# Every second pair of expert units loaded through POOL's queue instead of SyncE's

## The chip, the cores and the metric

The kernel runs on one core of a Trainium2 chip. The metric is the device time of one execution in microseconds; before the change it was 1349.06 us, the median of three runs (1348.57 to 1350.34). All data are fp32.

## The reference

One decoder layer on 256 tokens of width 1024: a mixer of three branches with an output projection, cross-attention to 256 memory tokens, and a mixture of experts, each followed by a residual sum and a LayerNorm. The change touches the mixture of experts alone:

```python
logits = hf @ router_w + router_b                # 32 experts, the top 4 of each token
act = clamped_swiglu(xb @ w_gu[e] + b_gu[e])     # w_gu[e]: 1024 x 2048
yb = act @ w_down[e] + b_down[e]                 # w_down[e]: 1024 x 1024
acc = acc.at[tok].add(yb * gate)
```

The weights of the 32 experts are 403 MB, and every expert is used, so all of them have to come from HBM once.

## The kernel before

The layer's dense part comes first (its weights are called raw when they are loaded, and whl when they are split into two parts). Then the experts run one after the other, each for up to 64 tokens. An expert's weights are cut into 12 **units** of 128 x 2048 numbers, 1.05 MB: units 12e to 12e+7 are for the up projection (two halves of four units, psum hp), 12e+8 to 12e+11 for the down projection (psum yp). PE reads the units strictly in their order, 0 to 383. Two neighbouring units that begin with an even number stand together in HBM as one block, a **pair**, and are loaded by one DMA of 128 rows of 16 KB, 2 MB (line 829).

A loaded unit stands in a **home**, a buffer in SBUF. The first 22 units (NF = 22) are placed by FIRST (line 87), partly during the dense part. From unit 22 on, later_chunks() (line 95) walks round the list WRAP (line 89): the homes ra0, ra1, re0, re1, rab, C, P, A and Q hold a pair each, the four of ONES (raw, two whl and rb) a single unit, and these four are left out from unit 120 on. So a round has 22 units at first and 18, nine pairs, later.

What sets the order of the loads: behind each unit's matmuls the program calls used(n) (line 1104). It takes the next loads off the list `waiting` as long as the home of the first one held no unit later than n, and hands each to chunk_load (line 817). The load is a DMA instruction in the order of the engine that issues it. There it waits until PE has really read the old units of the home, and, since there are eight semaphores for the landings of an engine's loads, until the load eight places before it on that engine has landed. All this stands on SyncE (SP): single units at line 827, the halves of units for the home raw and for the last four units at line 815, pairs at line 829.

POOL has little to do from the experts' beginning on: at expert 12 it loads the bias rows bd (lines 1431 and 1432), which the sums acc need at expert 14 (acc_bias, line 1263); at expert 16 stands overflow() (line 1275), a branch that is taken only when an expert has more than 64 tokens, with loads on POOL's queue inside (when it isn't taken, POOL brings the semaphores of its loads to where the branch would have left them, INC_SWDGE_SEM at line 1280); and in the last LayerNorm it does two instructions on the tile o. Every engine goes through the test of the branch.

Of the kernel before, what the change touches and what calls it, by code (L numbers as in the profile page):

```python
# [90 lines left out]
NF = 22  # L91
# [73 lines left out]
def trunk(ctx, tc, xT, xn, mem, wd, wm, bdn, par, rows, out, upto=None):  # L165
    nc = tc.nc
    clock = {"pe": 6.0, "dve": 4.0, "act": 4.0, "step": 0, "hold": 0}
    POOL, SP = nc.gpsimd, nc.sync
# [31 lines left out]
    wpair = wm.rearrange("(n j) p c -> n (j p c)", j=2).rearrange("n (p x) -> n p x", p=128)  # L200
# [587 lines left out]
    def src(n, a, b):  # L788

        o = (n % 2) * UW  # L790
        return wpair[n // 2, :, o + a:o + b]
# [9 lines left out]
    homes = {"rab": rab}  # L801

    def place(h, n, i):

        if h not in homes:
            homes[h] = new_home(h)
        t = homes[h]
        if h == "raw":
            ring[n] = t
        else:  # L810
            v = t if h in ONES else t[:, i]
            ring[n] = [v[:, k * D:(k + 1) * D] for k in range(2)]

    def half_load(n, k):
        SP.dma_start(out=ring[n][k], in_=src(n, k * D, (k + 1) * D))

    def chunk_load(h, units, fresh=True):
        if fresh:
            homes.pop(h, None)
        for i, n in enumerate(units):  # L820
            place(h, n, i)
        if h == "raw" or units[-1] >= NW - 4:
            for n in units:
                for k in range(2):
                    half_load(n, k)
        elif len(units) == 1:
            SP.dma_start(out=homes[h], in_=src(units[0], 0, UW))
        else:
            SP.dma_start(out=homes[h].rearrange("p j c -> p (j c)"), in_=wpair[units[0] // 2])

    def sigm(p, arg, o):
        ACT.activation(o, p, AF.Sigmoid, bias=pc("b_in", arg))
# [185 lines left out]
    for u in range(NU):  # L1018
        kind, arg = ORDER[u]
        if u in EARLY:  # L1020
            n, k = divmod(EARLY[u], 2)
            if k == 0:
                h, us = next((h, us) for h, us in FIRST if n in us)
# [73 lines left out]
    for h in ("raw", f"whl{S3}", f"whl{S2}", "rb", "A"):  # L1097
        chunk_load(*waiting.popleft())
# [5 lines left out]
    def used(n):  # L1104

        while waiting and holds[waiting[0][0]] <= n:
            h, us = waiting.popleft()
            chunk_load(h, us)
            holds[h] = us[-1]
# [65 lines left out]
    def ypt():  # L1175
        return mq.tile([128, 512], FP, name="yp", tag="yp")
# [165 lines left out]
    for e in range(NE):  # L1342
# [24 lines left out]
        if e == 0:  # L1367
            keep_warm(hp0, WARM[3])
            banks = [ypt(), misc("xgp"), hp1]

            def first(k):
                gather(xg, G, banks[k % 3], k, 1, (0, 1))

            first(0)
            first(1)
            chunk_load(*last_chunk)
            residual_rows(0)
            residual_rows(1)
            for k in range(8):
                up_part(hp0, xs, [ring[k // 2][k % 2]], [k])  # L1380
                if k < 6:
                    first(k + 2)
                if k % 2:
                    used(k // 2)
        else:
            for q in range(4):
                up(hp0, 0, q)
                if e == ROWS3_AT:
                    a, h = divmod(q, 2)
                    p = ypt()  # L1390
                    PE.matmul(p, ones, diag[:, 4 * q:4 * q + 4, :].rearrange("p n c -> p (n c)"), start=True, stop=True)
                    ACT.activation(r3[:, a, h * 512:(h + 1) * 512], p, AF.Copy)
# [3 lines left out]
        for q in range(4):  # L1396
# [5 lines left out]
            if e == NE - 1:  # L1402
                c, h = divmod(q, 2)
# [175 lines left out]
```

## Time and profile before

| | |
|---|---|
| median of three runs | 1349.06 us |
| the profiled execution | 1349.69 us |
| its span, first to last instruction | 1348.0 us |
| PE, DVE, ACT busy | 1274.3, 539.2, 427.4 us |
| POOL busy | 7.6 us |
| moved by DMA | 478.87 MB, 355 GB/s over the span |
| of it SP's queue (q1) | 474.41 MB in 54416 packets |
| of it POOL's queue (q0) | 2.76 MB in 784 packets |

One execution was profiled. Its span lies inside its own time; what remains is before the first and after the last instruction. A busy PE is not a PE at its peak, since matmuls overlap. The page also cuts the span into 40 slices and gives, for each, the busy share of the engines and what the DMA moved; a window query gives the same for any stretch. The chain is followed back from the last instruction: at each step to what released it. A DMA in the chain lasts from its issue to its landing. "DMA share" is the mean busy share of the core's 16 DMA engines.

### The profile page before, as it was taken

How to read it: one execution, taken by the hardware profiler on the slowest of the kernel's cores; microseconds unless marked ns; L12 is line 12 of the kernel's file. 1: busy time of each engine (PE TensorE's matmuls, PEld its weight loads, DVE VectorE, ACT ScalarE, POOL GpSimd, SP SyncE). 2: the span in 40 equal slices, each digit the busy share in tenths (PEclk: the TensorE clock that was granted, in tenths of full speed). 3: DMA queues.
4: the chain of work that ended last, by engine and by line, in shares of the span. 5: the costliest groups of instructions: out<-in, count | busy, mean ns of one | idle time of the engine just before them, and what ended most of it. 6: DMA issues, size and time to landing. Idle time of an engine off the chain costs nothing. (4 is left out here: it accounts for less than half of the span.)

```text
span 1348.0 us, 17416 instructions
## 1 busy us (share of the span) xinstructions
PE 1274.3 (95%) x7063; PEld 718.0 (53%) x7064; DVE 539.2 (40%) x1022; ACT 427.4 (32%) x841; POOL 7.6 (1%) x30
## 2 busy tenths in 40 slices
PE   9999999999999999999999989899999998889896
PEld 8999799988896343343333333343343333333332
DVE  6898889868754322222122121212222122222213
ACT  6878798764654111111111111112111011111101
POOL 0000000000000000000000000000000000000000
PEclk9999999999999999999999998999999999999998
DMA  6766576467679999999999999999999999999994
GB/s 213 238 205 231 188 236 201 144 197 242 235 257 378 409 428 426 427 425 423 419 428 428 426 429 427 426 426 428 427 428 428 428 426 428 428 428 427 427 427 169
DMA packets 55574, 478.87 MB, mean 355 GB/s; under 512 B 6560, under 2 KB 6816, under 8 KB 31424
## 3 DMA queue, kind: packets, MB, share of 16 engines
q1 hardware_dynamic: 54416, 474.41, 87.7%
q0 software_dynamic: 784, 2.76, 0.6%
q8 instruction: 58, 0.95, 0.3%
q10 hardware_dynamic: 288, 0.52, 0.1%
q14 instruction: 28, 0.23, 0.0%
HBM read 476.61 MB, written 1.05 MB: 354 GB/s over the span
## 5 line engine op out<-in xcount | busy, mean ns | idle before, releaser
L160 PE MATMUL hp<-ring,xg 128*64 128x512 f32 x2040 | 458.6, 597 | 20.3 <-DMA ring<-in_wm 16.6
L160 PEld LDWEIGHTS hp<-ring,xg 128*64 128x64 f32 x2040 | 143.7, 137 | 302.6 <-issue 267.1
L160 PE MATMUL yp<-ring,act 128*64 128x512 f32 x1016 | 239.6, 603 | 19.1 <-DMA ring<-in_wm 18.6
L160 PE MATMUL pd<-x_hl,whl 128*128 128x256 f32 x1896 | 232.0, 284 | 1.3 <-ACT whl L160 1.3
L160 DVE TENSOR_TENSOR hb<-hT,par 128x512 f32<-128x512 f32 x64 | 44.3, 692 | 471.1 <-PE hT L160 459.1
L160 PEld LDWEIGHTS pd<-x_hl,whl 128*128 128x128 f32 x1896 | 229.1, 192 | 2.2 <-ACT whl L160 1.9
L160 DVE TENSOR_TENSOR whl<-raw,whl 128x1024 fp32r<-128x1024 f32 x117 | 142.9, 1222 | 41.6 <-ACT whl L160 40.7
L160 PEld LDWEIGHTS yp<-ring,act 128*64 128x64 f32 x1016 | 67.6, 137 | 143.8 <-issue 140.4
L160 ACT ACTIVATE whl<-raw 128x1024 fp32r<-128x1024 f32 x117 | 123.5, 1056 | 48.4 <-DMA raw<-in_wd 21.3
L160 ACT ACTIVATE hs<-hp 128x256 f32<-128x256 f32 x128 | 42.1, 381 | 274.0 <-PE hp L160 274.0
L160 ACT ACTIVATE sg<-hb 128x256 f32<-128x256 f32 x64 | 26.7, 417 | 259.9 <-DVE hb L160 259.9
L160 ACT ACTIVATE cprod<-u,par 128x256 f32<-128x256 f32 x198 | 85.0, 498 | 0.0
L160 DVE COPY ys<-yp 64x512 f32<-64x512 f32 x31 | 21.5, 693 | 155.1 <-ACT ys L160 155.1
L160 PE MATMUL hp<-G,yn 128*128 128x128 f32 x488 | 59.0, 279 | 12.8 <-DVE G L160 12.8
L160 PEld LDWEIGHTS hp<-G,yn 128*128 128x128 f32 x488 | 55.8, 192 | 27.6 <-DVE G L160 26.0
L160 DVE TENSOR_TENSOR q_t<-q_t,cprod 128x512 f32<-128x512 f32 x99 | 65.5, 686 | 1.0
L160 PE MATMUL acc<-ys,GT 128*128 128x512 f32 (+1 forms) x128 | 60.0, 607 | 0.0
L160 PEld LDWEIGHTS hT<-ident,hs 128*128 128x128 f32 x256 | 26.8, 140 | 51.9 <-issue 50.3
L160 ACT ACTIVATE xg<-hp,lnp 128x128 f32<-128x128 f32 x62 | 28.4, 458 | 71.3 <-PE hp L160 56.9
L160 DVE TENSOR_SCALAR xg<-hp,lnp 128x128 f32<-128x128 f32 x60 | 24.6, 410 | 62.0 <-ACT xg L160 62.0
L160 ACT ACTIVATE ys<-yp 64x512 f32<-64x512 f32 x31 | 18.3, 590 | 91.1 <-PE yp L160 91.1
L160 PEld LDWEIGHTS acc<-ys,GT 128*128 128x128 f32 (+1 forms) x128 | 22.7, 189 | 36.3 <-issue 36.3
(221 smaller groups left out, 836.5 us busy)
## 6 DMA issues: line engine op xcount, KB each, us to landing
ring<-in_wm SPq DMA_DIRECT2D x173, 2048.0 KB, 36.2
raw<-in_wd SPq DMA_DIRECT2D x130, 512.0 KB, 4.2
ring<-in_wm SPq DMA_DIRECT2D x42, 512.0 KB, 8.1
ring<-in_wm SPq DMA_DIRECT2D x15, 1024.0 KB, 21.3
rab<-in_wm SPq DMA_DIRECT2D x4, 512.0 KB, 5.6
memn<-in_mem SPq DMA_DIRECT2D x1, 1024.0 KB, 7.2
q_t<-in_xn POOLq DMA_DIRECT2D x1, 1024.0 KB, 6.1
rab<-in_rows POOLq DMA_DIRECT2D x2, 512.0 KB, 7.8
```

Source lines behind the costliest of these rows:

```text
L160: return f(*args, **kw)
```

## The change

In chunk_load, a pair from unit 22 on whose first number doesn't divide by 4 is issued by POOL; the pairs with 24, 28, 32 and so on stay on SP, and so do single units, half units and the first 22 units.

```diff
         elif len(units) == 1:
             SP.dma_start(out=homes[h], in_=src(units[0], 0, UW))
         else:
-            SP.dma_start(out=homes[h].rearrange("p j c -> p (j c)"), in_=wpair[units[0] // 2])
+            queue = POOL if units[0] >= NF and units[0] % 4 else SP
+            queue.dma_start(out=homes[h].rearrange("p j c -> p (j c)"), in_=wpair[units[0] // 2])
```

## Rows read from the trace of the kernel before

**Rows 1.** The page: busy time of the engines, share of the span, instructions.

```profile
PE 1274.3 (95%) x7063; PEld 718.0 (53%) x7064; DVE 539.2 (40%) x1022; ACT 427.4 (32%) x841; POOL 7.6 (1%) x30
```

**Rows 2.** Stretches: length, engines' busy time, PE clock, DMA share, GB/s.

```profile
455.00:640.00 185.00, 180.26 (x878) 71.18 (x876) 43.01 (x101) 28.07 (x69) 0.00 (x0) 1.00 1.01 424
...
670.00:860.00 190.00, 178.56 (x824) 67.12 (x820) 39.41 (x94) 25.49 (x64) 0.00 (x0) 0.98 1.01 427
860.00:1020.00 160.00, 152.77 (x709) 60.42 (x708) 35.72 (x92) 24.00 (x58) 0.00 (x0) 0.99 1.01 427
1020.00:1314.00 294.00, 264.44 (x1246) 100.23 (x1244) 59.69 (x140) 37.83 (x93) 0.00 (x0) 1.00 1.01 427
```

**Rows 3.** DMA from 1020 to 1300 us: queues; issues, us to landing.

```profile
DMA packets 8219, 119.71 MB, mean 428 GB/s; under 512 B 911, under 2 KB 911, under 8 KB 911
...
q1 hardware_dynamic: 8207, 119.54, 100.4%
q8 instruction: 9, 0.15, 0.2%
...
ring<-in_wm SPq DMA_DIRECT2D x53, 2048.0 KB, 39.1
```

**Rows 4.** SP's waits, 455 to 1286 us: total us, times, longest.

```profile
SPq L829 <- DMA ring<-in_wm: 381.7, 113, 5.0
SPq L829 <- PE hp L160: 173.9, 65, 7.6
```

**Rows 5.** The chain that ended last: start, us, what.

```profile
1278.43 36.99 DMA ring<-in_wm
...
1328.39 7.04 PE yp L160 x32
```

**Rows 6.** SP's issues of ring loads: ns (minimum, median, maximum).

```profile
L829 SPq DMA_DIRECT2D ring<-in_wm x173: 327/328/424, 417.3 to 1281.9; - x173
```

**Rows 7.** The timeline of POOL: start, us, instruction.

```profile
407.96 0.53 POOL L1061 DMA_DIRECT2D gain<-in_rows  x1 [73.59 <-DMA ring<-in_wm]
```

**Rows 8.** The timeline of SP from 428 to 431 us.

```profile
429.15 0.33 SPq L829 DMA_DIRECT2D ring<-in_wm  x1
```

**Rows 9.** DMA from 430.5 to 433.5 us: packets, MB, share.

```profile
q1 hardware_dynamic: 71, 0.90, 76.2%
```

**Rows 10.** DMA issues over the whole span: KB, us to landing.

```profile
raw<-in_wd SPq DMA_DIRECT2D x130, 512.0 KB, 4.2
...
q_t<-in_xn POOLq DMA_DIRECT2D x1, 1024.0 KB, 6.1
...
gain<-in_rows POOLq DMA_DIRECT2D x1, 512.0 KB, 8.2
```

**Rows 11.** DMA from 411.7 to 415.8 us, both queues at work.

```profile
DMA packets 311, 1.75 MB, mean 428 GB/s; under 512 B 33, under 2 KB 33, under 8 KB 161
...
q1 hardware_dynamic: 167, 1.23, 71.0%
q0 software_dynamic: 144, 0.52, 31.3%
```

**Rows 12.** The tile bd: who reads it, and its loads.

```profile
L160 PE MATMUL acc<-bd,gT x8: 589/688/1057, 832.9 to 836.9; 33*128 33x512 f32 x8
...
DMA to landing us min/median/max: 7.3/7.7/8.1
```

**Rows 13.** Line 1280, the branch, on POOL: ns, first and last start.

```profile
L1280 POOLq COMPARE_BRANCH  x1: 45/45/45, 651.8 to 651.8; - x1
L1280 POOLq INC_SWDGE_SEM  x1: 293/293/293, 659.7 to 659.7; - x1
```

**Rows 14.** The timeline of PE near the end.

```profile
1307.61 7.04 PE L160 MATMUL hp<-ring,xg 128*64 128x512 f32 x32
1315.47 1.94 PE L160 MATMUL hp<-ring,xg 128*64 128x512 f32 x8 [0.82 <-DMA ring<-in_wm]
...
1321.89 1.94 PE L160 MATMUL hp<-ring,xg 128*64 128x512 f32 x8
```

## The prediction

> **What bounds the kernel now.** I read four views, in this order. First the page and its stretches [rows 1, 2]: PE looks busy throughout, but from 455 to 1314 us the DMA engines are busy all the time too, at 424 to 427 GB/s. A share of 1.01 means that each of the 16 engines has one packet behind the other; nothing is left between them. PE is at 97% up to 640 us and at 90% from 1020 us on (264.4 of 294 us). So PE sets the pace first, while it uses up what was loaded ahead, and the DMA sets it later. An expert is 12 units of 1.05 MB, 12.58 MB, or 29.4 us at the 428 GB/s of the late stretch [rows 3]; PE's own work in it is 90% of that, 26.5 us, so PE makes up some 2.9 us per expert when it is late.
>
> Second the loads [rows 3, 4]: in the late stretch a 2 MB load lands 39.1 us after its issue although it takes 4.9 us (2.10 MB at 428 GB/s), so eight are always in flight. SP waits 381.7 us, 113 times, for an earlier load of its own before it may issue the next one, and 174 us for PE's hp matmuls alone to release a home. Those waits cost nothing: eight loads are in flight meanwhile.
>
> Third the chain that ended last [rows 5]: loads, a little PE, loads again. Its last load, units 376 and 377, is issued at 1278.43 and has landed at 1315.42; behind it are six units (378 to 383), 6.29 MB, so the last byte lands 14.7 us later, at T = 1330.1. PE ends the last yp matmul at 1328.39 + 7.04 = 1335.4, 5.3 us after T; then come the last LayerNorm and the stores, which the change leaves alone. **The end is T plus what PE still has to do when the last units land.** The change can move the time only by moving T, or by changing the order in which the last units land.
>
> **The change, part by part.** Of the 171 later pairs (173 issues on line 829 [rows 6], less 18/19 and 20/21), 86 go to POOL, 22/23 to 378/379, and 85 stay on SP, along with the single units and the half units of the last four. The buffers, the bytes and PE's order stay.
>
> *Issuing.* 86 issues of 0.33 us leave SP [rows 6] and come to POOL at some 0.5 us each [rows 7]. POOL is busy for 7.6 us of 1348 [rows 1], so this costs nothing; the backlog of eight loads hides it. The wait of SP for its own loads gets shorter or goes; what is late next is the DMA engines, which are full. Gain: 0.
>
> *The first load on POOL.* At 429.15 SP issues 22/23 [rows 8] when the backlog is nearly gone: the engines are filled to 76% in the 3 us from 430.5 [rows 9]. Here an issue's latency is bare and moves T. SP's 512 KB load lands after 4.2 us, POOL's 1 MB load after 6.1 us [rows 10]; the additional 512 KB take 1.2 us at 428 GB/s, which leaves 0.7 us. POOL's 512 KB gain load took 8.2 us beside SP's loads, 4.0 more than 4.2. Bounds 0 and 4.0; I take 0.7, as the 1 MB load is the nearest thing to ours. The loads after it find the engines at work. The Trainium skill (DMA: Bandwidth & Descriptors, Specifications) gives POOL's path about 1 us to the first byte and SP's 0.6; by that the term would be an estimated 0.4 and the sum 2.6. The trace shows landings, not first bytes, and agrees in the sign.
>
> *Steady state.* When POOL loaded the gain row, both queues ran at once: in 4.1 us POOL's queue had 144 packets and SP's 167, together 428 GB/s [rows 11]. So the two queues take turns packet by packet, and the total stays. POOL's 128 packets of 4 KB took 31.3% of 16 x 4.1 us, 160 ns each. I take the same rate for POOL's 16 KB rows: 0 us, with both ends in the rivals.
>
> *POOL's own waits.* A POOL load waits until PE has used its home; behind it on POOL stand bd (experts 12 to 14), the branch at expert 16 and the o instructions of the last LayerNorm, which are far off. bd is now issued at expert 12, two experts (58.8 us) before the acc matmul at 832.9 needs it [rows 12], behind at most four POOL loads at half rate, 4 x 9.8 us, plus its own 8.1 [rows 12]: 47 us, cover 11 us. If the cover is gone PE waits, and makes it up by its 10% later. At the branch POOL waits for all its loads before INC_SWDGE_SEM [rows 13]; today it has only bd's two loads in flight, which land within 7.3 to 8.1 us [rows 12], and it stands from 651.8 to 659.7. After the change it will have about four loads in flight and issues nothing for up to 39 us (eight shared loads of 4.9). SP's loads keep the DMA full, so T does not move; PE gets POOL's next pair some 12 us late (a shared load of 9.8 and the latency) and makes that up within five of the 15 experts left. Cost 0, if the two streams close up again.
>
> *Early units.* Up to unit 119 SP has 12 to 14 of every 22 units but only every second turn, and its single units have shorter packets, so POOL runs ahead there and PE will wait for SP. PE's idle time from 670 to 1314 us is 11 + 7 + 30 = 48 us [rows 2], which covers such waits. Cost 0.
>
> *The end.* Two loads that share the engines take 9.8 us each and land close together, where they landed 4.9 us apart. PE needs 374 (POOL's) before 376 (SP's). If 376 lands when it does now, 374, now at 1310.5 (4.9 before it), may come x later, x between 0 and 4.9. PE starts 374 at 1311.1 (half of the 7.04 us from 1307.61 [rows 14]) and needs 3.5 us for it; 376 starts at 1315.47 after 0.82 us of waiting. With x the start of 376 becomes 1310.5 + x + 3.5, or x - 1.5 later: 0 to 3.4 us. I take x = 3.7, three quarters, as POOL's stream starts late at the first load and again after the branch: 2.2 us.
>
> **Sum:** 0.7 + 0 + 0 + 2.2 = +2.9 us. The profiled execution took 1349.69 us (span 1348.0), 0.63 over the median of 1349.06; it becomes 1352.6, and the median **1352.0**. Own range 0 to +7.4. About 0.2%, 2.7 us, is what a measurement can tell from no change.
>
> **Rivals.**
> *1. The streams drift apart.* Nothing ties POOL's stream to SP's; uneven packets and the wait at the branch push them apart by a pair or more. POOL behind: 378 lands at T, PE has from 1321.89 to 1335.4 to do after it [rows 5, 14], 13.5 us instead of 5.3, +8.2; with 374 at T - 4.9, 1335.4 - 1311.1 - 0.8 = 23.5 us after it, +13.3. POOL ahead: SP's 372, 376 and 380 to 383 come last, 372 at T - 14.7 with 27.0 us of PE behind it, +7.0. For it: the early stretch and the branch. Against: a queue that is ahead runs out of free homes and leaves its turns to the other. I take +9, 1358.
> *2. POOL's packets are slower.* If its rows go out in 4 KB packets, four take 640 ns where a 16 KB row takes 612 (4.9 us / 8): 4.6% of 86 x 4.9 us, +19, and POOL's share of the turns falls, +9 more. If they are 1% slower, +4. For it: no row shows a 16 KB row on POOL's queue. Against: its 4 KB packets run at full rate [rows 11]. The Trainium skill (DMA: Bandwidth & Descriptors, Latency and other measured facts) guesses that POOL's descriptor rings crowd the ports of engines 7 and 15. Rows 11 show no such slowness, with few packets.
> *3. Faster.* With packets of two queues at hand an engine overlaps the end of one with the start of the next. For it: in rows 11 the shares add up to 102.3%, in the late stretch to 100.6% [rows 3]. The 1.7% belong to packets of 0.24 us on average (102.3% of 65.6 us by 311 less 33 short ones); with 612 ns it would be 0.67% of the 880 us from 450 us to T, -6 us, 1343, and PE, which waits for the DMA from 1020 us on, would follow. It decides as soon as the steady rate passes 428 GB/s by more than 0.3%. Against: small packets alone may do that.
> *4. All is hidden.* The pairs land in the same order a little shifted, 1349.
>
> **Chances.** Forecast 0.52; drift 0.22; slow packets 0.12; faster 0.09; hidden 0.05. The forecast's middle lies just over the 0.2% line, so 0.27 of it counts as slower and 0.25 as the same. Slower 0.27 + 0.22 + 0.12 = 0.61, same 0.25 + 0.05 = 0.30, faster 0.09. The range runs from 1346 (half a faster case's gain) to 1364 (a drift of 13.3 on a late start); left out are most of case 3 and the upper half of case 2.
>
> **What would show it.** Right: two queues of about 183 MB and 294 MB, 427 to 428 GB/s in the late stretch; POOL loads that land after about as long as SP's; a stretch after 870 us in which POOL issues nothing; T within 1.5 us; PE's last wait moved to a POOL pair and the yp matmuls ending 2 to 4 us later. Wrong: another rate in the late stretch (cases 2, 3), one queue empty while the other has eight in flight, or the last SP units landing long after the last POOL pair (case 1). The forecast falls if PE no longer waits for the DMA at the end, or the DMA engines stand idle in mid-kernel.

## The result: 11 us slower, nearly all of it after the last byte

The kernel after takes 1360.18 us (median of four runs, 1359.55 to 1361.57) against 1348.82 us for the kernel before beside it: a ratio of 1.0085, 95% interval 1.0073 to 1.0098. A second set of five runs gave 1360.43 against 1348.79, 1.0093 (1.0080 to 1.0107). The profiled execution took 1359.55 us, with a span of 1357.8 (before 1348.0).

The page of the kernel after, its busy engines and its queues (they answer to rows 1):

```profile
PE 1279.2 (94%) x7063; PEld 719.7 (53%) x7064; DVE 539.2 (40%) x1022; ACT 427.1 (31%) x841; POOL 53.2 (4%) x116
...
q1 hardware_dynamic: 42032, 294.05, 55.6%
q0 software_dynamic: 13168, 183.12, 32.0%
```

The change does what it says: 183 and 294 MB, and POOL is busy for 46 us more with its 86 issues of 0.53 us, which stand in nobody's way. The stretches of rows 2 and the late DMA of rows 3, after:

```profile
455.00:640.00 185.00, 178.10 (x866) 70.27 (x864) 42.32 (x100) 27.48 (x68) 9.03 (x17) 1.00 1.01 425
670.00:860.00 190.00, 186.83 (x868) 71.31 (x866) 41.07 (x97) 26.61 (x66) 11.64 (x22) 0.99 1.01 425
860.00:1020.00 160.00, 149.12 (x682) 57.24 (x680) 36.30 (x94) 23.05 (x55) 8.48 (x16) 0.98 1.01 427
1020.00:1314.00 294.00, 269.55 (x1254) 103.83 (x1252) 59.70 (x140) 38.48 (x95) 14.84 (x28) 0.98 1.01 427
```

```profile
q0 software_dynamic: 4106, 59.67, 50.2%
q1 hardware_dynamic: 4103, 59.79, 50.1%
...
ring<-in_wm SPq DMA_DIRECT2D x28, 2048.0 KB, 29.4
ring<-in_wm POOLq DMA_DIRECT2D x28, 2048.0 KB, 40.6
```

The DMA engines are as full as before and move as much, to within 2 GB/s. But look at the last column of the issues: a POOL pair lands 40.6 us after its issue, an SP pair after 29.4, where all took 39.1 [rows 3]. The queues take equal turns, and POOL's holds the longer backlog: **its pairs come late**.

PE near the end, kernel after (answers to rows 14 and 5):

```profile
1299.47 3.65 PE L160 MATMUL hp<-ring,xg 128*64 128x512 f32 x16 [0.71 <-DMA ring<-in_wm]
...
1334.23 7.09 PE L160 MATMUL yp<-ring,act 128*64 128x512 f32 x32
```

and POOL's closing instructions, three DRAINs that stand behind the last instruction that the program writes, kernel before and kernel after (ns: minimum, median, maximum of the three; first and last start):

```profile
L1575 POOLq DRAIN  x3: 40/112/1882, 1341.8 to 1347.7; - x3
```

```profile
L1576 POOLq DRAIN  x3: 50/104/8907, 1347.7 to 1357.2; - x3
```

In the kernel before the last byte lands at T = 1330.30, the yp matmuls end at 1335.41, and the span ends 12.60 us later. After, T is 1331.64, the yp matmuls end at 1341.32, and the span ends 16.50 us later. So the 9.8 us of the span are 1.34 at T (of which 0.69 were there before the change has any part: 18/19, the first pair of line 829 and still SP's, is issued at 418.01 instead of 417.32), **4.57 between T and the end of the yp matmuls, and 3.90 behind them**. That last part is the DRAIN on POOL: the first of three takes 8.91 us instead of 1.88, follows POOL's two instructions on o, and the span ends 1.2 us behind it. Before, it was over at 1343.7, hidden under the stores.

The branch (rows 13), after, on POOL, and POOL's timeline around it:

```profile
L1281 POOLq COMPARE_BRANCH  x1: 54/54/54, 864.2 to 864.2; - x1
...
L1281 POOLq INC_SWDGE_SEM  x1: 1171/1171/1171, 898.9 to 898.9; - x1
```

```profile
863.61 0.53 POOL L830 DMA_DIRECT2D ring<-in_wm  x1 [7.82 <-PE yp L160]
900.66 1.59 POOL L830 DMA_DIRECT2D ring<-in_wm  x3 [36.53 <-DMA ring<-in_wm]
```

POOL issues nothing from 863.61 to 900.66, 37 us. From here on I follow one number, the **offset**: when a POOL pair lands, less when the SP pair behind it in PE's order lands, plus the 4.9 us by which they landed apart before; 0 is the old order, above 0 POOL is behind. It comes from the issue and landing of each ring load. In the kernel after it is between -21 and -37 at units 62 to 118 (POOL ahead, as SP carries the single units), -7.3 at 138 to 158, -3 at 178 to 198, and +10.5 from unit 210 to 370, with a dip to 9.0 at 286 to 302: the pause at the branch put POOL two pairs behind, and nothing shortened that. "At the end" below means the value up to unit 366.

### The profile page after: what moved, and what is told of

It reads as the page before. It is cut to its first block, busy times and chain, and to the rows that moved or that the text cites. A ratio compares the mean times of both kernels' runs of the same rounds, so it can differ in the third digit from the quotient of the medians.

```text
span 1357.8 us, 17414 instructions
## 1 busy us (share of the span) xinstructions
PE 1279.2 (94%) x7063; PEld 719.7 (53%) x7064; DVE 539.2 (40%) x1022; ACT 427.1 (31%) x841; POOL 53.2 (4%) x116
## 4 chain that ended last, share of the span: by engine, by line
PE 48%; issue 26%; DMA 14%; DVE 5%; ACT 3%; POOL 1%; another core or an unknown queue 1%; SPq 0%; POOLq 0%; DVEq 0%; ACTq 0%
PE hp L160 17%; PE pd L160 16%; DMA ring<-in_wm 11%; PE yp L160 7%; PE acc L160 5%; DMA raw<-in_wd 3%; POOL ring L830 1%; ACT cprod L160 1%; PE hT L160 1%; ACT whl L160 1%; DVE q_t L160 1%; DVE whl L160 1%; DVE hb L160 1%; PE sc L160 1%
## 5 line engine op out<-in xcount | busy, mean ns | idle before, releaser
L160 PE MATMUL hp<-ring,xg 128*64 128x512 f32 x2040 | 467.8, 608 | 38.9 <-DMA ring<-in_wm 34.2
L830 POOL DMA_DIRECT2D ring<-in_wm x86 | 45.6, 531 | 825.5 <-PE hp L160 521.6
L160 PE MATMUL hp<-G,yn 128*128 128x128 f32 x488 | 59.0, 279 | 12.8 <-DVE G L160 12.8
```

The lines of the kernel that those rows point to most:

```text
L160: return f(*args, **kw)
L830: queue.dma_start(out=homes[h].rearrange("p j c -> p (j c)"), in_=wpair[units[0] // 2])
```

## Experiments

The theory after the comparison: (A) the steady state costs nothing, and the loss is in the order in which the last pairs land, and in POOL's closing DRAIN, which grows with the number of loads that POOL issued. Rival B: sharing costs something all along (drift, PE's waits, contention). All medians below are beside runs of the kernel before on the same chip: 1349.37 for experiments 1 to 3, 1348.94 for 4 to 7, 1348.44 for 8 to 10, 1348.79 for 11.

**1. The kernel after without the branch.**

```diff
-        if e == OVER_AT:
-            overflow()
```

> The changed kernel without the branch at expert 16 (the extra pass for experts with more than 64 tokens, which these inputs never take, is left out). If POOL's wait at the branch is what puts its stream behind, POOL's pairs keep their place there (2.8 us early before it, instead of 10.5 us late behind it), and the last yp matmul ends 1 to 3 us after that of the kernel before without the branch, instead of 5.9 us. If two streams cost this whatever their order, or POOL's packets are slower, it stays 5 to 6 us. The closing drain on POOL, 8.9 us with the branch: if it takes some 82 ns for every load POOL has issued (7.0 us more for 86 loads), 8.9 us again; if only for the loads since the branch, 163 ns for each of 43, it grows to some 16 us.

1356.49 (ratio 1.0060, 1.0043 to 1.0077), 7.1 us over before instead of 11.4. The offset is -1.4 at the end, the step to +10.5 is gone; still the yp matmuls end 9.29 us after T, 4.2 more than before where 1 to 3 were expected, and the DRAIN takes 8.91 us. So the branch makes the step, and the DRAIN doesn't depend on it: it counts all 86 loads, not those since the branch. The same edit to the kernel **before** shows what the branch itself costs:

> The control of the last one: the kernel before without the branch. The DMA engines set the end, so the last byte should land at 1330 us as before and the time stay within 1 us of 1348.8; PE's 4 us at the branch were made up anyway. If PE's lateness at expert 16 counted, it would be 4 to 7 us faster.

1348.38, ratio 0.9998 (0.9988 to 1.0007): nothing.

**2. The step undone by half a pair.**

```diff
+        elif units[0] == 214:
+            POOL.dma_start(out=homes[h][:, 0, :], in_=src(214, 0, UW))
+            SP.dma_start(out=homes[h][:, 1, :], in_=src(215, 0, UW))
```

> The changed kernel with one pair (units 214 and 215, the second one after the branch) shared out: 214 through POOL's queue, 215 through SP's, 1 MB each. That shortens POOL's list by half a pair and lengthens SP's by as much, 4.9 us of shared loading on each side, so that POOL's lateness of 10.5 us should fall to about 0.7 us and stay there. If the offset of the streams is the cost, the last yp matmul ends 1.3 to 2.5 us later than in the kernel before instead of 5.9, and the time is 1355 to 1357. If the cost lies in POOL's queue as such, the time stays at 1360. The closing drain stays near 8.9 us with both.

1356.85 (1.0060, 1.0039 to 1.0082). The pair behind the branch that would be POOL's is split between the queues, and the offset at the end is -0.6. This is the forecast's own case, two streams in step. PE's last waits there:

```profile
1298.23 1.94 PE L160 MATMUL yp<-ring,act 128*64 128x512 f32 x8 [1.93 <-DMA ring<-in_wm]
1317.71 1.94 PE L160 MATMUL hp<-ring,xg 128*64 128x512 f32 x8 [0.79 <-DMA ring<-in_wm]
```

The second is the start of 376, as in rows 14; T is 1329.67, so it begins at T - 11.96 where it began at T - 14.83 before, 2.9 us later, and the yp matmuls end 7.98 us after T instead of 5.11, 2.9 later. Two loads are in flight at equal turns: when the first has landed, half of the next is in, so the last pairs land closer to T than one by one (374 at T - 17.5 instead of T - 19.8, 376 at T - 12.0 instead of T - 14.9).

**3. o on DVE in the kernel after**, so that POOL is done early and its DRAIN can start early.

```diff
-    on(POOL, 0, 0, OP.mult)
-    on(POOL, 0, 1, OP.add)
+    on(DVE, 0, 0, OP.mult)
+    on(DVE, 0, 1, OP.add)
```

> The changed kernel with the two o instructions of the last LayerNorm on DVE instead of POOL. POOL then has nothing to do after its last load and can drain beside PE's last 18 us. DVE's own work grows by 2 x 0.7 us. If the closing drain of 8.9 us is what adds 3.9 us to the end, the span ends some 4.5 us after the last output store is issued, as before, and the time falls by 2 to 3 us to about 1357.5. If something else of the end is late (the stores, SP's waits), it gets 0 to 1.4 us slower, 1360 to 1361.5.

1357.97 (1.0057, 1.0036 to 1.0078). The DRAIN starts at 1290.5, while POOL's last loads are still on their way (378 lands at 1321.8), and ends at 1325.6, out of the way. The yp matmuls are followed by 13.7 us instead of 16.5; of the 1.1 left over 12.6, the two instructions on o, 1.42 us on DVE, are the likely cause. In this execution the offset was +12.8 and the yp matmuls ended 12.34 us after T, so the end that was won stands beside a worse tail.

**4. The DRAIN alone.** The kernel before, all weights on SP, with 86 additional loads of 1 KB on POOL where the change puts its pairs.

```diff
+            if units[0] >= NF and units[0] % 4:
+                POOL.dma_start(out=pt[0:16, PC["conv_a"] + 200:PC["conv_a"] + 216], in_=par[0:16, 0:16])
```

> The kernel before, all pairs on SP, with an added load of 1 KB on POOL's queue (16 rows of 64 bytes into columns that are no longer read) wherever the changed kernel would load a pair through POOL: 86 loads without weights. If the closing drain counts POOL's loads, it takes 8.9 us as in the changed kernel and the span ends about 3.8 us later, 1352 to 1353, with the last byte and the yp matmuls as before. If it goes by bytes or packets, the drain stays at 1.9 to 2.5 us and the time at 1349.

1353.31 (1.0033, 1.0022 to 1.0043), 4.4 us above before. The yp matmuls end 4.67 us after T, as before; POOL's closing DRAIN:

```profile
L1577 POOLq DRAIN  x3: 50/112/8906, 1341.7 to 1351.2; - x3
```

8.91 us again, and 16.17 us from the yp matmuls to the end, 3.6 more than before. 86 KB in place of 180 MB make the same DRAIN: it goes with the **number** of loads. (The other 0.8 us would be at T, which in this profile lies 1.8 us farther from the issue of 18/19; it was not followed.)

**5. The same sharing with ACT's queue in place of POOL's.**

```diff
-            queue = POOL if units[0] >= NF and units[0] % 4 else SP
+            queue = nc.scalar if units[0] >= NF and units[0] % 4 else SP
```

> The changed kernel with ACT's queue in POOL's place: the same pairs on a second queue, but no load on POOL. ACT has to wait for PE's reads before it issues, between its own instructions. The closing drain on POOL and POOL's wait at the branch are gone; what is left of the cost is the sharing. Expected: drain 1.9 us, no step of the offset at expert 16, yp end 8 us after the last byte (5.1 with one queue), time 1352 to 1353. If POOL's queue as such, not the sharing, made the tail late, 1349 to 1350. If ACT's waits hold up its copies of hp and yp, PE loses time in every expert and the time goes beyond 1360.

1356.64 (1.0055, 1.0038 to 1.0072). POOL's DRAIN is back at 1.88 us and the end behind the yp matmuls at 12.60. But ACT's stream runs ahead by 14 us, so SP's pairs are late, and the yp matmuls end 13.22 us after T, where 8 were expected. The loads from 1150 to 1300 us show which queue is behind:

```profile
ring<-in_wm ACTq DMA_DIRECT2D x15, 2048.0 KB, 24.8
ring<-in_wm SPq DMA_DIRECT2D x14, 2048.0 KB, 38.8
```

So the DRAIN is POOL's, and the late tail comes with ACT's queue as well.

**6. POOL up to unit 299 only.**

```diff
-            queue = POOL if units[0] >= NF and units[0] % 4 else SP
+            queue = POOL if NF <= units[0] < 300 and units[0] % 4 else SP
```

> The changed kernel with POOL taking its pairs only below unit 300; the last 20 of its 86 go back to SP. If the tail is late because two loads in flight share the engines, so that each of the last pairs lands when half of the next one is on chip too (2.3 to 2.9 us late with streams in step, more with POOL behind), it is gone here: the yp matmuls end 5.1 us after the last byte as in the kernel before, not 9.7. The closing drain on POOL at 82 ns for each of 66 loads over 1.9 us: 7.3 us, which still sets the end by some 2 us; time 1352 to 1353. If POOL's loads as such cost (lost DMA time or PE time), the last byte would be late and the time 1355 or more. If the drain goes by the time since POOL's last load, it is under 2 us and the time 1350.

1350.27 (1.0010, 1.0001 to 1.0020). Early drift, branch and step are all there (an offset of +10 up to unit 294), but the last pairs come from one queue, and the yp matmuls end 4.61 us after T. 66 loads make a DRAIN of 7.27 us; 14.53 us behind the yp matmuls, 1.9 more than before, are what is left. The time is 2 us below what was expected, and an offset of +10 for 80 units of mid-kernel costs nothing that can be told.

**7. POOL from unit 120 on**, without the stretch of single units.

```diff
-            queue = POOL if units[0] >= NF and units[0] % 4 else SP
+            queue = POOL if units[0] >= ONES_TO and units[0] % 4 else SP
```

> The changed kernel with POOL taking pairs only from unit 120 on (65 of 86), where SP has no single units any more. POOL's lead of up to 36 us in the first ten experts and PE's wait of some 10 us in expert 8 should be gone. If PE's later idle time covers that wait, as the prediction has it, the last byte, the yp end 9 to 10 us after it and POOL's lateness of 10 us behind the branch stay, and only the closing drain gets shorter, 1.9 + 65 x 0.082 = 7.2 us: 1357 to 1358.5. If the early disorder is carried to the end, the time falls below 1356.

1354.97 (1.0042, 1.0025 to 1.0059). This is below the 1357 to 1358.5 that were expected if the early stretch left no trace. The early stretch was not the only source of drift: POOL's queue, which begins empty beside eight SP loads, is 39 us ahead at once. That lead shrinks to 14.6 at unit 198, and from there to unit 214, across the branch, the offset rises by 12.7, to -1.9 (in the kernel after by 13.8, from -3.3 to +10.5). So the branch adds about the same in both, and the offset that stood before it counts. The end has an offset of -3.2, yp matmuls 9.95 us after T, and a DRAIN of 7.19 us for 65 loads.

**8. POOL from unit 300 on.**

```diff
-            queue = POOL if units[0] >= NF and units[0] % 4 else SP
+            queue = POOL if units[0] >= 300 and units[0] % 4 else SP
```

> The kernel after, with POOL loading every second pair only from unit 300 on (20 loads). Theory A (the time is lost in the order in which the last pairs land, and in POOL's closing DRAIN, which takes 1.9 us and 82 ns more for each load that POOL has issued; the shares in mid-kernel cost nothing): the two queues start in step, two pairs land close together, the yp matmuls end 8 to 10 us after T as in the runs with an offset of 0 to -3 (5.1 before), the DRAIN is 1.88 + 20 x 0.082 = 3.5 us and hidden. 2.9 to 4.8 us more than before: 1352 to 1354. Rival B (each shared pair costs the same, 11.2 us / 86 = 0.13 us): 1351.6, with the yp matmuls ending about 5 us after T. Rival C (the DRAIN alone): 1349.

1360.78 (1.0081, 1.0067 to 1.0095): all expectations missed. I had let the streams begin in step; after experiment 7 that was wrong. With 20 loads on POOL the loss is that of 86. The DRAIN takes 3.52 us and is hidden (12.37 us behind the yp matmuls). POOL's stream jumps 41 us ahead and is still 20 ahead at the end; SP's pairs are late. Loads from 1150 to 1300 us, then PE's last wait:

```profile
ring<-in_wm SPq DMA_DIRECT2D x15, 2048.0 KB, 38.4
ring<-in_wm POOLq DMA_DIRECT2D x15, 2048.0 KB, 16.9
```

```profile
1308.12 3.23 PE L160 MATMUL yp<-ring,act 128*64 128x512 f32 x8 [2.05 <-DMA ring<-in_wm]
```

This is 368, SP's, landed 21.1 us before T (1329.04), where it landed 34.5 before T in the kernel before. The yp matmuls end 19.13 us after T: 13.4 us late in landing, 14.0 late at the end.

**9. POOL in the middle only**, 42 loads.

```diff
-            queue = POOL if units[0] >= NF and units[0] % 4 else SP
+            queue = POOL if ONES_TO <= units[0] < 290 and units[0] % 4 else SP
```

> The kernel after, with POOL loading every second pair only from unit 120 to 289 (42 loads), so that the branch and the drift are there, but the last 47 pairs are SP's. Theory A: yp matmuls end about 5 us after T, the DRAIN takes 1.88 + 42 x 0.082 = 5.3 us and ends when SP's closing part does: 1349, with 1348.5 to 1350 allowed. Rival B (0.13 us for each shared pair): 1354.5, by a later T or by gaps of the DMA.

1348.62, ratio 0.9997 (0.9988 to 1.0006): **the whole loss is gone**, and rival B with it. The streams drift here too: POOL is 39 us ahead at first, 13 ahead before the branch and still 1.4 ahead after it. That a POOL stream that is late costs nothing in mid-kernel either is shown by experiment 6. PE's waits from 640 to 860 us, this kernel and then before, and from 1020 to 1345 us, in the same order:

```profile
PE yp L160 <- DMA ring<-in_wm: 12.8, 5, 6.2
PE hp L160 <- DMA ring<-in_wm: 2.7, 4, 0.8
...
PE yp L160 <- DMA ring<-in_wm: 8.5, 7, 1.3
PE hp L160 <- DMA ring<-in_wm: 7.8, 10, 1.4
```

```profile
PE yp L160 <- DMA ring<-in_wm: 5.2, 4, 1.3
PE hp L160 <- DMA ring<-in_wm: 3.2, 5, 0.8
...
PE yp L160 <- DMA ring<-in_wm: 13.4, 10, 1.4
PE hp L160 <- DMA ring<-in_wm: 12.9, 17, 1.2
```

7.1 us more in the middle, 10.0 less later: waits were moved, not added. The DRAIN is 5.31 us, from 1341.5 to 1346.8, just inside the stores:

```profile
L1576 POOLq DRAIN  x3: 50/104/5309, 1341.5 to 1347.5; - x3
```

**10. A shorter end in the kernel before**: pairs from unit 324 on as two loads of 1 MB.

```diff
+        elif units[0] >= 324:
+            for i, n in enumerate(units):
+                SP.dma_start(out=homes[h][:, i, :], in_=src(n, 0, UW))
```

> The kernel before, with every pair from unit 324 on loaded by two DMAs of 1 MB on SP. If the end is T plus what PE has left when the last pairs land, the first unit of a pair can be multiplied 2.45 us earlier (1.05 MB at 428 GB/s), and PE, which needs 26 to 27 us for an expert that takes the DMA 29.4, gets up to that far ahead in five experts: yp matmuls end 2.7 to 4.3 us after T (5.1 before), 1346.6 to 1348.2. Rival: rows of 8 KB move more slowly (424 against 427 GB/s where single units are loaded early on, 0.7% of 60 x 2.46 us = 1.0 us) and PE's waits for the pair were not what counted: 1349 to 1350.

1348.07, ratio 0.9995 (0.9986 to 1.0004): no change that can be told. The yp matmuls end 2.54 us after T, 2.6 better, as the equation of the end has it; but T came 2.9 us later from the issue of 18/19 on. The stretch from 1150 to 1314 us, this kernel and the one before:

```profile
1150.00:1314.00 164.00, 150.68 (x706) 56.42 (x704) 33.78 (x79) 21.36 (x52) 0.00 (x0) 1.00 1.01 422
```

```profile
1150.00:1314.00 164.00, 148.47 (x701) 56.80 (x702) 33.78 (x79) 21.36 (x52) 0.00 (x0) 1.00 1.01 427
```

Loads of 1 MB in rows of 8 KB move 1.2% more slowly here (0.7% was expected), 1.7 us on the 63 MB of these units. The other 1.2 us at T were not followed.

**11. The kernel after once more**, as its median lay 11.4 us over before and its profile gave 8.5 for the two terms.

> The kernel after once more, unchanged. The end of the yp matmuls (9.7 - 5.1 = 4.6 us after T) and the DRAIN (16.5 - 12.6 = 3.9 us) make 8.5 us of its profile, where its four runs stood 11.4 us over before. Theory A (these two terms are all, and the step at the branch is made alike in every execution): an offset of 9 to 12 us from unit 210 on, yp matmuls ending 9 to 11 us after T, 1357.5 to 1359.5. Rival (the offset is settled anew by small differences in each execution, and with it the end): another offset, yp matmuls ending 8 to 14 us after T, 1356 to 1362.

1360.43 (1.0093, 1.0080 to 1.0107). Now the offset is +12.8 and the yp matmuls end 12.44 us after T: 7.3 + 3.9 = 11.2 us, near what the medians show. The step differs between executions, as the rival of this run has it (12.8 in experiment 3, 10.2 in experiment 6). The two profiled executions took nearly the same time, though, 1359.55 and 1359.83, as T itself stood 2.4 us earlier in this one, and so it is not shown that the first profile was a light one.

The offset is not all of the 2.8 us between the two tails. PE's last wait of this execution, for 366 as in the line from 1299.47 above:

```profile
1298.10 5.35 PE L160 MATMUL hp<-ring,xg 128*64 128x512 f32 x16 [2.00 <-DMA ring<-in_wm]
```

366 begins 1.1 us closer to T than in the first profile. The other 1.7 us are PE's: the same 16 matmuls take 5.35 us instead of 3.65, and the granted clock is 0.50 from 1298.5 to 1301.8, the lower of its two levels (1.2 GHz), where it was 1.00 from 1299.5 to 1302.8 in the first profile. Such a fall to 0.50 stands behind PE's last wait for a load, of about 2 us, in experiments 1, 3, 7 and 8 too, and is part of the yp column below in these runs. It doesn't always come: in experiment 5 the clock stays at 1.00 behind a wait of 2.07 us, and in experiment 2 behind one of 1.93. A late pair can thus cost twice, by the wait and by the clock behind it.

The runs side by side (us; "behind" is from the last yp matmul to the end of the span):

| run | loads on 2nd queue | offset at the end | yp end after T | DRAIN | behind | median over before |
|---|---|---|---|---|---|---|
| before | 0 | none | 5.11 | 1.88 | 12.60 | 0 |
| after | 86 | +10.5 | 9.68 | 8.91 | 16.50 | +11.4 |
| after again (11) | 86 | +12.8 | 12.44 | 8.90 | 16.49 | +11.6 |
| half pair (2) | 86 | -0.6 | 7.98 | 8.91 | 16.50 | +7.5 |
| no branch (1) | 86 | -1.4 | 9.29 | 8.91 | 16.12 | +7.1 |
| from 120 (7) | 65 | -3.2 | 9.95 | 7.19 | 14.45 | +6.0 |
| o on DVE (3) | 86 | +12.8 | 12.34 | early | 13.70 | +8.6 |
| ACT (5) | 86 | -14 | 13.22 | 1.88 | 12.60 | +7.7 |
| from 300 (8) | 20 | -20 | 19.13 | 3.52 | 12.37 | +12.3 |
| to 299 (6) | 66 | none | 4.61 | 7.27 | 14.53 | +1.3 |
| 120 to 289 (9) | 42 | none | 5.09 | 5.31 | 12.71 | +0.2 |
| 1 KB loads (4) | 86 | none | 4.67 | 8.91 | 16.17 | +4.4 |

Two columns make the time: what the yp column and "behind" lie over before adds up to the last column within 1.5 us, but for the first profile of after. The DRAIN is 1.88 us and 82 ns for each load on POOL, (8.91 - 1.88) / 86, and the runs with 20, 42 and 65 loads lie on that line. Up to 42 loads it is hidden.

## Why the prediction was right, and what it missed

The direction and the range (1346 to 1364) hold, and 1360.2 is 8.2 us over the number. The sum itself doesn't hold: its own range was 0 to +7.4, and the change costs 11.4. What holds is the wide range, which was drawn around rival 1. The streams did drift apart, at a lower price than the rival gave for POOL behind, and a DRAIN that nothing in the prediction held makes up the rest; that the time lies inside is in part luck. Of the signs named for the forecast, T (1.3 us later) and a last wait for a POOL pair came; POOL's loads land later than SP's, and the yp matmuls end 5.9 us later instead of 2 to 4.

- *Steady state, 0*: right. 427 GB/s and a share of 1.01 in the late stretch, two queues at half each, and experiment 9. With it rivals 2 and 3 fall: POOL's packets are neither slower nor better packed. The trouble at engines 7 and 15 that the Trainium skill (DMA: Bandwidth & Descriptors, Latency and other measured facts) suspects would show as a lower rate; none of these runs shows it.
- *Issuing, 0*: right; SP's wait for its own loads got shorter, as said. In the stretch of rows 4 it falls from 381.7 to 223.1 us at the pairs' line, and the wait for PE's hp matmuls, which the prediction didn't name here, rises from 173.9 to 283.0:

```profile
SPq L830 <- PE hp L160: 283.0, 50, 12.1
...
SPq L830 <- DMA ring<-in_wm: 223.1, 48, 9.4
```

- *The first load on POOL, 0.7*: not shown. In the first two profiles the pair 22/23 lands 9.6 us after POOL's issue and 9.3 after SP's. Over all executions profiled it is 9.0 to 11.8 us from POOL and 9.3 to 10.4 from SP, so the term can't be told from nothing, and neither can the estimated 0.4 by the Trainium skill's first-byte figures (DMA: Bandwidth & Descriptors, Specifications). T moved by 0.65 from the issue of 18/19 on; over the executions profiled that distance varies by more (912.2 to 915.4 us in those with full pairs).
- *Early units, 0*: right, for the reason given. POOL ran some 30 us ahead and PE waited for SP at expert 8, 8.6 us in the stretch from 640 to 700 us where it had waited for no load before; experiments 6 and 9 show that such waits are won back.
- *bd, 0*: right. Its loads land after 30.3 us (47 were allowed), at 809, and the acc matmul that needs them starts at 837.4:

```profile
L160 PE MATMUL acc<-bd,gT x8: 589/589/693, 837.4 to 840.5; 33*128 33x512 f32 x8
...
DMA to landing us min/median/max: 29.9/30.3/30.6
```

- *The branch, "Cost 0, if the two streams close up again"*: the first step that failed. The pause was right (37 us, 39 allowed), but the streams did not close up. PE made up the late pairs, as the step said; the late stream stayed late, because two backlogs at equal turns keep their distance (10.4 to 10.6 us at units 210 to 282). It costs some 4 us: after stands 11.4 us over before, experiment 1 only 7.1 and experiment 2 only 7.5.
- *The end, 2.2*: the assumption "If 376 lands when it does now" is the second step that failed. With the streams in step it is 376 itself that starts 2.9 us later (experiment 2), so the size was near and inside the bounds 0 to 3.4; with POOL behind, PE's last wait is for 366 already. 366 in the kernel before:

```profile
1290.96 3.65 PE L160 MATMUL hp<-ring,xg 128*64 128x512 f32 x16 [0.50 <-DMA ring<-in_wm]
```

  After, the wait ends at T - 32.2 where 366 began at T - 39.3 before, 7.2 us later. From there PE does its 18 units without a wait, in 41.85 us instead of 44.45, and so wins back 2.6: 4.6 us. In the second execution profiled it was 7.3, with 1.7 of it from the lower clock. PE's 10% wins back a wait in mid-kernel; with one and a half experts left there is no time for that.
- *"then come the last LayerNorm and the stores, which the change leaves alone"*: the third, and the one that no term or rival held. It is true of the instructions written in the program. Behind them stands POOL's closing DRAIN, which the kernel before ends in time: 3.9 us, 3.6 alone in experiment 4.
- *Rival 1, the drift*: it came, with POOL behind, and the price is 4.6 to 7.3 us instead of 8.2 to 13.3. I had POOL's last pair land at T; but SP still had eight half units to issue, so 378 landed 8.9 us before T, and the late pair that counts stood earlier. "A queue that is ahead runs out of free homes and leaves its turns to the other" was no protection: it brought the offset from -29 to -3 and then let +10.5 stand. POOL ahead, +7.0, is what experiments 5 and 8 made (8.1 and 14.0).

No version here beats the kernel before: it keeps the DMA full, experiment 9 equals it, and experiment 10 is the same within the noise. A split of only the last few pairs was not run.

## What to carry to other kernels

Where one queue keeps the DMA engines full, a second queue adds no bytes; it gives up the order of landing, and that order is worth the most where nothing behind it can win time back: keep the last loads on one queue, in the order of their use. When loads move to POOL, read what the engines do behind the last line of the program, not only the stores, and count POOL's DMAs there. In this kernel a pause on one of two sharing queues was not repaired by itself: follow the landing of neighbouring loads on both, and compare the queues' times from issue to landing.

## What the runs showed that I had not expected

- POOL's DRAIN at the end of the program takes 1.9 us with the few loads of the kernel before and 82 ns more for each load that POOL issued, 1 KB or 2 MB alike. INC_SWDGE_SEM at the branch grows as well, from 0.29 to 1.17 us.
- A queue that begins empty beside a queue with eight loads in flight overtakes it by about 40 us (experiments 7, 8 and 9), because from its first load on it has half of the turns. That lead shrinks later, but not to nothing.
- Two queues that share, neither of them empty, keep their offset to within 0.2 us for dozens of units (after, 210 to 278 and 306 to 370), while its size differs between executions of one program (10.5 and 12.8 us).
- In five of the executions profiled, PE's last wait of about 2 us for a late load was followed by a stretch at a granted clock of 0.50; in experiment 11 the 16 matmuls behind it took 1.7 us longer for it.
